# Feature sums and mean subtraction of the last layer norm, moved to TensorE for one column range

## The chip, the cores and the metric

The kernel runs on one core of a Trainium2 chip. The metric is the device time of one execution in microseconds (us). A NeuronCore has a matrix engine (TensorE, PE in the profile, with its weight loads listed as PEld), three engines for elementwise work (VectorE or DVE, ScalarE or ACT, GpSimd or POOL), and queues that issue transfers (SP is the main one here). Each engine runs its own list of instructions in order; semaphores make one wait for another.

## What is computed

One transformer-like layer (three parallel mixing heads, an output projection, layer norm, a SwiGLU feed-forward block, layer norm), for 1024 prompt tokens and 32 sample tokens with 1024 features. The change touches only the very last step, the second layer norm:

```python
def _layer_norm(x, g, b):
    xf = x.astype(jnp.float32)
    mu = xf.mean(-1, keepdims=True)
    var = jnp.square(xf - mu).mean(-1, keepdims=True)
    return ((xf - mu) * lax.rsqrt(var + LN_EPS) * g + b).astype(x.dtype)
...
    y = (jax.nn.silu(h @ w_gate) * (h @ w_up)) @ w_down
    x = _layer_norm(ALPHA * x + (1 + g2) * y, ln2_g, ln2_b)
```

The sums run over the 1024 features of each token.

## The kernel before, in words

Activations lie transposed: features on the 128 partitions, tokens along the free dimension. The 1024 features are eight feature tiles, called m or k below, from 0 to 7. The 1056 tokens are two groups: group 0 has tokens 0 to 511, group 1 has the other 544. Group 1 is worked in two column ranges of 272 tokens, (0, 272) and (272, 544). The array `z` holds the residual sum of a group, eight tiles of 272 columns for each range.

The matrix products use a two-part split of each operand (high and low part), so that each product of 128x128 weights with 272 columns is three matmuls (lines 117 to 119, `gemm`). These operands have the type fp32r. A matmul on plain fp32 operands, as the norm uses, shows in the profile as two matmul records.

The tail of the program is the loop at lines 1453 to 1469. It goes through the two column ranges in the order (272, 544), then (0, 272). For each it makes the last part of the up projection (`up`, line 1016), the last part of the down projection (`down`, line 1162) and the norm (`ln2`, line 1177).

`down` goes through the eight feature tiles in the order 4, 5, 6, 7, 0, 1, 2, 3. For each it issues twelve matmuls into a PSUM bank (tags "g" and "gu" in turn, three banks each) and then calls `sublayer_end` (line 951). There VectorE adds the gated product to `z` (line 960), and `ln_sum` (line 849) collects the sums of the norm:

- ScalarE squares the tile (line 853 for the first, line 856 for the others);
- GpSimd adds the tile to `zs`, the sum of the features (line 860);
- VectorE adds the square to `qs`, the sum of squares (line 862).

In the second range, (0, 272), the last two tiles of the order, 2 and 3, are "late": they are not added on GpSimd and VectorE but kept in a list (line 858) for TensorE.

`ln_means` (line 864) then sums over the partitions. TensorE multiplies `onesm`, a 128x128 matrix with 1/1024 in each place, with `zs` and with the kept tiles for the mean, and with `qs` and the kept squares for the mean square (line 872): six fp32 matmuls in the second range, two in the first. The results are `pm` and `pq`, in two PSUM banks of the tag "t".

`ln2` forms the variance on VectorE (line 1187) from `pq` and the square of `pm` (ScalarE, line 1185), copies `pm` to SBUF as `mean` (ScalarE, line 1186), and gets `r`, one over the deviation, from `ln_rstd` (lines 879 to 883: a logarithm and an exponential on ScalarE, then three VectorE steps). VectorE takes the mean off tile after tile (`less`, line 1189) and multiplies by `r` (`scaled`, line 1205). The first three `less` steps are placed right behind the variance; each later one is placed behind the `scaled` step of the tile before. Last comes the affine step with gain and offset, on ScalarE (line 1207), or for tile 7 of the last range on VectorE (line 1209). Tiles are stored (line 1212) in pairs 0-1, 2-3 and 4-5 and then singly, from SP's queue, except tile 6 of the last range, which goes from ScalarE's queue.

While `down` works on the second range, `weave` and the argument `turns` let the norm of the first range run tile by tile between its steps. The order of instructions on an engine is made ahead of the run by a planner that takes the program's order as priority and moves up a later instruction where an earlier one isn't ready by its own estimate. `issue_after` holds an instruction behind a named one of the same engine.

Of the kernel before, what the change touches and what calls it, by code (L numbers as in the profile page):

```python
# [7 lines left out]
F32 = mybir.dt.float32  # L8
F32R = mybir.dt.float32r
AF = mybir.ActivationFunctionType  # L10
ALU = mybir.AluOpType
# [4 lines left out]
P = 128  # L16
D = 1024
KT = 8
# [38 lines left out]
def weave(*parts):  # L57

    parts = list(parts)
    while parts:  # L60
        for p in list(parts):
            if next(p, parts) is parts:
                parts.remove(p)
# [6 lines left out]
class Kernel:  # L70
# [10 lines left out]
    def t(self, pool, shape, dt=F32, tag=None, bufs=None):  # L81
        self.n += 1
        kw = {} if bufs is None else {"bufs": bufs}
        return pool.tile(shape, dt, tag=tag, name=f"{self.phase}_{tag}_{self.n}", **kw)
# [751 lines left out]
    def ln_begin(self, eng, pivot=True, sum=True):  # L836
        t = lambda tag: self.t(self.pn, [P, 544], F32, tag, 2)
        return {"zs": t("zs"), "qs": t("qs"), "pv": t("pv"), "eng": eng, "pivot": pivot, "sum": sum,
                "order": range(KT), "late": (), "rest": []}

    def ln_pivot(self, st, z, sl):
        nc = self.nc
# [6 lines left out]
    def ln_sum(self, st, z, m, sl):  # L849
        nc = self.nc  # L850
        o = st["order"]
        if m == o[0]:
            nc.scalar.activation(st["qs"][:, sl], z[:, m, sl], AF.Square)
            return
        sq = self.t(self.p2, [P, 272], F32, "tmp", 4)[:, :sl.stop - sl.start]
        nc.scalar.activation(sq, z[:, m, sl], AF.Square)
        if m in st["late"]:
            st["rest"].append((z[:, m, sl], sq))
            return
        st["eng"].tensor_tensor(st["zs"][:, sl], z[:, o[0], sl] if m == o[1] else st["zs"][:, sl],  # L860
                              z[:, m, sl], ALU.add)
        nc.vector.tensor_tensor(st["qs"][:, sl], st["qs"][:, sl], sq, ALU.add)

    def ln_means(self, st, sl):


        out = []
        for i, x in enumerate(("zs", "qs")):
            p = self.t(self.pt, [P, 512], F32, "t")[:, :sl.stop - sl.start]
            parts = [st[x][:, sl]] + [y[i] for y in st["rest"]]  # L870
            for n, y in enumerate(parts):
                self.nc.tensor.matmul(p, self.onesm, y, start=n == 0, stop=n == len(parts) - 1)
            out.append(p)
        st["rest"] = []
        return out
# [301 lines left out]
    def ln2(self, c, st, a, b, aff, late=False):  # L1177

        self.phase = f"lnb{c}"
        nc, z, sl = self.nc, self.z[c], slice(a, b)  # L1180
        eng = {"p": nc.gpsimd, "v": nc.vector}
        pm, pq = self.ln_means(st, sl)
        mean = st["zs"][:, sl]
        v = self.t(self.p2, [P, 272], F32, "tmp", 4)[:, :b - a]
        nc.scalar.activation(v, pm, AF.Square)
        nc.scalar.copy(mean, pm)
        first = nc.vector.scalar_tensor_tensor(v, pq, self.epsa, v, ALU.add, ALU.subtract)
        r = st["pv"][:, sl]
        less = lambda k: nc.vector.tensor_tensor(z[:, k, sl], z[:, k, sl], mean, ALU.subtract)
        scale = self.ln_rstd(r, v)  # L1190
        if late:
            with self.tc.issue_after(first.ins):
                for k in range(3):
                    less(k)
        yield
        for k in range(KT):
            self.phase = f"lnb{c}"
            zk = z[:, k, sl]
            g, o = self.colp[:, 64 + k:65 + k], self.colp[:, 72 + k:73 + k]
            if not late:  # L1200
                less(k)
            elif k >= 3:
                with self.tc.issue_after(scaled.ins):
                    less(k)
            scaled = nc.vector.tensor_tensor(zk, zk, r, ALU.mult)
            if aff[k] == "a":
                nc.scalar.activation(zk, zk, AF.Identity, bias=o, scale=g)
            else:
                eng[aff[k]].tensor_scalar(zk, zk, g, o, ALU.mult, ALU.add)
            k0 = k if k >= 6 and c else k - k % 2  # L1210
            if k % 2 or k0 == k and k >= 6 and c:
                (nc.scalar if k in self.scq else nc.sync).dma_start(
                    self.d["o_yT"][k0:k + 1, :, GO[c] + a:GO[c] + b].rearrange("k p n -> p k n"), z[:, k0:k + 1, sl])
            yield
# [15 lines left out]
    def run(self):  # L1230
        nc, tc, d = self.nc, self.tc, self.d
        dr = self.pool("dr", space=DRAM)
        t = lambda shape, tag: self.t(dr, shape, F32, tag)
# [49 lines left out]
        sl = ExitStack()  # L1283
        self.pl = self.pada = self.pool("pl", ctx=sl)
        w1 = d["w_in_v"]
        rest = list(range(16, 20)) + list(range(8, 16))
# [71 lines left out]
        st = self.ln_begin(nc.gpsimd)  # L1358
# [18 lines left out]
        for g, (j0, nj) in enumerate(GROUPS):  # L1377
# [30 lines left out]
            if g == WOB - 1:  # L1408
                st = self.ln_begin(nc.gpsimd, sum=False)
# [20 lines left out]
        for g, (j0, nj) in enumerate(GROUPS):  # L1430
# [13 lines left out]
            if g < last:  # L1444
                st = self.ln_begin(nc.gpsimd, sum=False) if g == last - 1 else None
# [3 lines left out]
        n = nj * 256  # L1449
        t = self.t(self.pz, [P, 4, n], F32R, "z0", 1)  # L1450
        w = self.last_weights(((t[:, 0], t[:, 1]), (t[:, 2], t[:, 3])), (2, 3))
        act2 = dict(act)
        for half, (a, b) in enumerate(LN[1][::-1]):
            if half == 0:
                wt = {j: self.up_weights(j) for j in range(FF - TS, FF)}
            for j in range(FF - TS, FF):
                weave(self.up(1, j, (act, act2)[half], pa, ((a, b),), wt[j]))
            if half:
                st["late"] = st["order"][6:]
            else:  # L1460
                h, l = (self.t(pb, [P, KT * 272], F32R, f"{x}{a}", 1) for x in ("ah", "al"))
                w.update(self.last_weights(((h[:, :n], l[:, :n]), (h[:, n:2 * n], l[:, n:2 * n])), (0, 1)))
            self.down(1, last, (act, act2)[half], ((a, b),), st, w, end if half else iter(()))
            self.scq = (6,) if half else ()
            end = self.ln2(1, st, a, b, TAFF[half], True)
            if half:
                weave(end)
            else:
                next(end)
# [103 lines left out]
```

## Time and profile before

| quantity | value |
| --- | --- |
| time, median of 3 runs | 1392.73 us (1391.56 to 1393.49) |
| the profiled execution: time | 1390.37 us |
| the profiled execution: span, first to last instruction | 1388.5 us |
| mean granted TensorE clock | 0.993 of full speed |
| TensorE matmul busy | 1345.2 us, 97% |
| VectorE busy | 1034.2 us, 74% |
| ScalarE busy | 641.3 us, 46% |
| GpSimd busy | 259.1 us, 19% |

In the views quoted below a row of the timeline gives the start in us from the start of the span, the duration in us, the engine, the line, the operation, the tile written, the tiles read, the shapes and a count; a bracket names the idle time before it and what ended it. Rows with a count above one are merged: the duration then reaches from the first start to the last end. Starts of rows in line can lie closer than a duration, since an engine begins one instruction while the last drains; the distance from start to start is called the pitch below. Prefixes of tile names (`wo_z`, `sup_zs`, `lnb_t`) name the stage in which a buffer was made: `wo_z` is `z` of group 1, `sup_zs` and `sup_qs` are `zs` and `qs`, `sup_pv` is `r`, `lnb_t` is `pm` or `pq`, `dn_tmp` is a square.

### The profile page before, as it was taken

What the parts mean: (1) busy time and instruction counts of PE and PEld (TensorE: products, weight loads), DVE (VectorE), ACT (ScalarE), POOL (GpSimd) and SP (SyncE); (2) the same over time, 40 slices, a digit from 0 to 9 for tenths busy, and PEclk for the clock granted to TensorE, in tenths of its full rate; (3) what the DMA queues carried; (4) which work ended last, traced back from release to release, by engine and by line L of the source; (5) the groups of instructions that cost most, each with busy time, mean ns of one, the idle gap of its engine ahead of it and who ended that gap; (6) DMA issues with size and microseconds to landing.
All of it is one profiled execution on the core that took longest, in us unless ns stands there. A gap on an engine that the chain in (4) does not pass through costs nothing.

```text
span 1388.5 us, 25995 instructions
## 1 busy us (share of the span) xinstructions
PE 1345.2 (97%) x9683; PEld 1236.4 (89%) x9683; DVE 1034.2 (74%) x2214; ACT 641.3 (46%) x1261; POOL 259.1 (19%) x292
## 2 busy tenths in 40 slices
PE   7999999999999799999999999999999999999996
PEld 4899988899899778888887889899999999999996
DVE  5548656678689657777776766677898988888777
ACT  3323234444455444545544445335574544545355
POOL 0103200052157500000000000264610000000341
PEclk9999999999999899999999999999999999999998
DMA  9754577575665665444443442664497767453321
GB/s 362 266 211 134 176 242 212 187 237 149 212 205 160 180 184 182 125 131 137 133 135 86 108 127 81 195 169 134 157 229 195 216 163 214 136 175 115 101 90 65
DMA packets 136373, 233.09 MB, mean 168 GB/s; under 512 B 22564, under 2 KB 79532, under 8 KB 136248
## 3 DMA queue, kind: packets, MB, share of 16 engines
q1 hardware_dynamic: 130936, 221.34, 50.7%
q0 software_dynamic: 5168, 9.96, 4.7%
q8 instruction: 76, 1.25, 0.4%
q14 instruction: 49, 0.40, 0.1%
q10 hardware_dynamic: 144, 0.14, 0.0%
HBM read 197.50 MB, written 53.81 MB: 181 GB/s over the span
## 4 chain that ended last, share of the span: by engine, by line
PE 67%; DVE 5%; DMA 3%; ACT 1%; issue 1%; SPq 0%; POOL 0%; DVEq 0%; ACTq 0%
PE up_g L117 5%; PE up_g L118 5%; PE up_g L119 5%; PE dn_g L119 4%; PE dn_g L117 4%; PE dn_g L118 4%; PE sup_u L119 3%; PE sup_u L117 3%; PE sup_u L118 3%; PE wo_g L119 2%; PE wo_g L117 2%; PE wo_g L118 2%; PE sup_g L118 2%; PE sup_g L119 2%; PE sup_g L117 2%; PE fox_t L738 2%
## 5 line engine op out<-in xcount | busy, mean ns | idle before, releaser
L117 PE MATMUL up_g<-mlstm_ah,up_whi 128*128 128x512 f32 (+1 forms) x384 | 141.7, 369 | 4.4 <-ACT lna_tmp L981 3.3
L118 PE MATMUL up_g<-mlstm_al,up_whi 128*128 128x512 f32 (+1 forms) x384 | 142.1, 370 | 0.4 <-DVE mlstm_al L986 0.4
L119 PE MATMUL up_g<-mlstm_ah,up_wlo 128*128 128x512 f32 (+1 forms) x384 | 141.1, 368 | 0.0
L282 PE MATMUL tm_g<-tm_whi,start_h1h 128*128 128x256 f32 (+1 forms) x384 | 109.7, 287 | 1.5 <-ACT tm_mixs L633 1.5
L284 PE MATMUL tm_g<-tm_whi,start_h1l 128*128 128x256 f32 (+1 forms) x384 | 109.6, 287 | 0.0
L283 PE MATMUL tm_g<-tm_wlo,start_h1h 128*128 128x256 f32 (+1 forms) x384 | 109.5, 286 | 0.0
L117 PE MATMUL fm_g<-start_h1h,fm_whi 128*128 128x256 f32 (+2 forms) x344 | 101.7, 301 | 6.1 <-DVE fm_qkl L367 2.6
L118 PE MATMUL fm_g<-start_h1l,fm_whi 128*128 128x256 f32 (+2 forms) x344 | 100.8, 293 | 0.0
L119 PE MATMUL fm_g<-start_h1h,fm_wlo 128*128 128x256 f32 (+2 forms) x344 | 100.0, 292 | 0.0
L1105 ACT CAST sup_whi<-sup_raw 128x1024 fp32r<-128x1024 f32 x54 | 56.0, 1048 | 91.5 <-PE dn_u L118 47.9
L117 PEld LDWEIGHTS up_g<-mlstm_ah,up_whi 128*128 128x128 f32 x384 | 73.5, 192 | 16.7 <-ACT mlstm_ah L985 3.5
L118 PEld LDWEIGHTS up_g<-mlstm_al,up_whi 128*128 128x128 f32 x384 | 73.7, 192 | 12.3 <-DVE mlstm_al L986 1.5
L119 PEld LDWEIGHTS up_g<-mlstm_ah,up_wlo 128*128 128x128 f32 x384 | 73.8, 192 | 10.6
L105 ACT CAST up_whi<-up_raw 128x1024 fp32r<-128x1024 f32 x50 | 52.4, 1048 | 63.9 <-PE dn_g L118 25.1
L711 ACT ACTIVATE fox_p<-fox_s,fox_fmx 128x384 f32<-128x384 f32 (+2 forms) x96 | 55.0, 578 | 57.1 <-DVE fox_fmx L709 44.0
L282 PEld LDWEIGHTS tm_g<-tm_whi,start_h1h 128*128 128x128 f32 x384 | 72.2, 189 | 4.4 <-ACT tm_mixs L633 2.1
L117 PEld LDWEIGHTS fm_g<-start_h1h,fm_whi 128*128 128x128 f32 x344 | 64.7, 190 | 12.5 <-DVE fm_qkl L367 3.5
L1106 DVE TENSOR_TENSOR sup_wlo<-sup_raw,sup_whi 128x1024 fp32r<-128x1024 f32 x54 | 67.8, 1259 | 10.5 <-ACT sup_whi L1105 10.5
L106 DVE TENSOR_TENSOR up_wlo<-up_raw,up_whi 128x1024 fp32r<-128x1024 f32 x50 | 66.8, 1336 | 10.4 <-ACT up_whi L105 9.6
L284 PEld LDWEIGHTS tm_g<-tm_whi,start_h1l 128*128 128x128 f32 x384 | 72.2, 188 | 1.5 <-issue 1.2
L117 PE MATMUL dn_g<-up_acth,dn_whi 128*128 128x512 f32 (+2 forms) x200 | 73.5, 368 | 0.0
L118 PE MATMUL dn_g<-up_actl,dn_whi 128*128 128x512 f32 (+2 forms) x200 | 73.3, 368 | 0.0
(591 smaller groups left out, 4594.5 us busy)
## 6 DMA issues: line engine op xcount, KB each, us to landing
up_raw<-w_gu SPq DMA_DIRECT2D x50, 512.0 KB
dn_raw<-w_dn SPq DMA_DIRECT2D x28, 512.0 KB
ada_late<-w_ada SPq DMA_DIRECT2D x24, 512.0 KB
wo_raw<-w_o SPq DMA_DIRECT2D x24, 512.0 KB
sup_raw<-w_gu SPq DMA_DIRECT2D x20, 512.0 KB
start_dp<-w_gu SPq DMA_DIRECT2D x19, 512.0 KB
start_dp<-w_gu POOLq DMA_DIRECT2D x19, 512.0 KB, 7.8
sup_raw<-start_dp SPq DMA_DIRECT2D x18, 512.0 KB
```

Of the source, the lines that this page charges most:

```text
L105: nc.scalar.copy(hi[:, :w], raw[:, :w])
L106: (eng or nc.vector).tensor_tensor(lo[:, :w], raw[:, :w], f(hi[:, :w]), ALU.subtract)
L117: nc.tensor.matmul(ps, hi, xh(k), start=start and k == 0, stop=False)
L118: nc.tensor.matmul(ps, hi, xl(k), start=False, stop=False)
L119: nc.tensor.matmul(ps, lo, xh(k), start=False, stop=stop and k == n - 1)
L282: nc.tensor.matmul(ps[:, :ncol], xh, hi, start=k == 0, stop=False)
L283: nc.tensor.matmul(ps[:, :ncol], xh, lo, start=False, stop=False)
L284: nc.tensor.matmul(ps[:, :ncol], xl, hi, start=False, stop=k == 7)
L711: nc.scalar.activation(pr[:, lo:hi], banks[x][:, :hi - lo], AF.Exp, bias=mxs[:, 0:1], accum_out=sums[:, x:x + 1])
L738: nc.tensor.transpose(ps[:, c:c + P], probs[y][:, b * P:(b + 1) * P], self.ident)
L1105: nc.scalar.copy(h, x)
L1106: tt(l, x, f(h), ALU.subtract)
```

## The change

A flag `onpe` is set for the second range, (0, 272), alone. With it

- `ln_sum` no longer adds tiles on GpSimd. TensorE multiplies each tile with `onesm` and accumulates in one PSUM bank, `pm`, which is held from the first tile on. The matmul for a tile is issued after the product of the next tile.
- `ln_means` issues only the matmul of the last tile for the mean, and those of the mean square as before.
- `ln2` writes the mean with its sign turned. The first three tiles get the negative mean added on VectorE, as before with a subtraction. For tiles 3 to 7 TensorE forms the centred tile in a PSUM bank with two fp32 matmuls by the identity, one of the tile and one of the negative mean. VectorE's multiplication by `r` then reads that bank.
- For every range the copy of the mean is now an activation of the kind Copy with a scale of 1 or -1.

```diff
@@ ln_sum
         o = st["order"]
+        if st["onpe"]:
+            if m == o[0]:
+                st["pm"] = self.t(self.pt, [P, 512], F32, "t")[:, :sl.stop - sl.start]
+            for x in st["wait"]:
+                nc.tensor.matmul(st["pm"], self.onesm, x, start=x is st["first"], stop=False)
+            st["wait"] = [z[:, m, sl]]
+            if m == o[0]:
+                st["first"] = st["wait"][0]
...
-        st["eng"].tensor_tensor(st["zs"][:, sl], z[:, o[0], sl] if m == o[1] else st["zs"][:, sl],
-                              z[:, m, sl], ALU.add)
+        if not st["onpe"]:
+            st["eng"].tensor_tensor(st["zs"][:, sl], z[:, o[0], sl] if m == o[1] else st["zs"][:, sl],
+                                  z[:, m, sl], ALU.add)
         nc.vector.tensor_tensor(st["qs"][:, sl], st["qs"][:, sl], sq, ALU.add)
@@ ln_means
-        for i, x in enumerate(("zs", "qs")):
+        if st["onpe"]:
+            for n, x in enumerate(st["wait"]):
+                self.nc.tensor.matmul(st["pm"], self.onesm, x, start=False, stop=n == len(st["wait"]) - 1)
+            out.append(st["pm"])
+        for i, x in list(enumerate(("zs", "qs")))[len(out):]:
@@ ln2
-        nc.scalar.copy(mean, pm)
+        onpe = st["onpe"]
+        nc.scalar.activation(mean, pm, AF.Copy, scale=-1.0 if onpe else 1.0)
...
+        centred = {}
+        if onpe:
+            for k in range(3, KT):
+                p = centred[k] = self.t((self.pg, self.pu)[k % 2], [P, 512], F32, self.utag[k % 2])[:, :b - a]
+                nc.tensor.matmul(p, self.ident, z[:, k, sl], start=True, stop=False)
+                nc.tensor.matmul(p, self.ident, mean, start=False, stop=True)
...
-            elif k >= 3:
+            elif k >= 3 and not onpe:
                 with self.tc.issue_after(scaled.ins):
                     less(k)
-            scaled = nc.vector.tensor_tensor(zk, zk, r, ALU.mult)
+            scaled = nc.vector.tensor_tensor(zk, centred.get(k, zk), r, ALU.mult)
@@ run
             if half:
                 st["late"] = st["order"][6:]
+                st["onpe"] = True
```

More of the change, by code (lines that the diff above doesn't have):

```diff
@@ L838, in ln_begin @@
         return {"zs": t("zs"), "qs": t("qs"), "pv": t("pv"), "eng": eng, "pivot": pivot, "sum": sum,
-                "order": range(KT), "late": (), "rest": []}
+                "order": range(KT), "late": (), "rest": [], "onpe": False, "wait": [], "first": None}
     def ln_pivot(self, st, z, sl):
@@ L1185, in ln2 @@
         nc.scalar.activation(v, pm, AF.Square)
-        nc.scalar.copy(mean, pm)
+        onpe = st["onpe"]
+        nc.scalar.activation(mean, pm, AF.Copy, scale=-1.0 if onpe else 1.0)
         first = nc.vector.scalar_tensor_tensor(v, pq, self.epsa, v, ALU.add, ALU.subtract)
         r = st["pv"][:, sl]
-        less = lambda k: nc.vector.tensor_tensor(z[:, k, sl], z[:, k, sl], mean, ALU.subtract)
+        less = lambda k: nc.vector.tensor_tensor(z[:, k, sl], z[:, k, sl], mean, ALU.add if onpe else ALU.subtract)
         scale = self.ln_rstd(r, v)
```

## The prediction

> **What bounds the kernel now.** First the page's head, then a table of stretches of the last 35 us (each engine's busy us and count, the granted clock, DMA share, GB/s).
>
> ```profile
> span 1388.5 us, 25995 instructions
> PE 1345.2 (97%) x9683; PEld 1236.4 (89%) x9683; DVE 1034.2 (74%) x2214; ACT 641.3 (46%) x1261; POOL 259.1 (19%) x292
> ...
> 1354.00:1366.00 12.00, 12.00 (x95) 11.84 (x94) 9.26 (x24) 6.59 (x15) 1.69 (x3) 1.00 0.07 25
> 1366.00:1373.00 7.00, 7.00 (x57) 6.89 (x55) 7.00 (x14) 4.07 (x10) 3.97 (x5) 1.00 0.28 100
> 1373.00:1377.06 4.06, 3.65 (x13) 2.03 (x12) 2.10 (x5) 1.57 (x5) 0.19 (x1) 1.00 0.10 34
> 1377.06:1385.70 8.64, 0.00 (x0) 0.00 (x0) 8.32 (x21) 5.04 (x10) 0.00 (x0) 0.71 0.25 85
> ```
>
> TensorE is busy for 97% of the span, and through all 19 us of the last products; only then does it thin out and stop. So the stretch has three parts: products, on TensorE; sums, to 1377.06; normalising, on VectorE (8.32 of 8.64 us), and a last store. What TensorE is given before 1373 lengthens the program; what VectorE is relieved of after 1377 can shorten it. TensorE's timeline shows the hinge and the price of an fp32 matmul.
>
> ```profile
> 1358.05 0.62 PE L872 MATMUL lnb_t<-sup_zs,start_onesm 128*128 128x272 f32 x2
> 1358.50 0.62 PE L872 MATMUL lnb_t<-sup_qs,start_onesm 128*128 128x272 f32 x2
> ...
> 1372.82 0.28 PE L119 MATMUL dn_u<-up_acth,up_al 128*128 128x272 f32 x1
> 1373.24 0.73 PE L872 MATMUL lnb_t<-sup_zs,start_onesm 128*128 128x272 f32 x2
> 1374.85 0.72 PE L872 MATMUL lnb_t<-sup_qs,start_onesm 128*128 128x272 f32 x2 [0.17 <-DVE sup_qs L862]
> 1375.41 0.62 PE L872 MATMUL lnb_t<-dn_tmp,start_onesm 128*128 128x272 f32 x2
> 1375.87 0.62 PE L872 MATMUL lnb_t<-wo_z,start_onesm 128*128 128x272 f32 x2
> 1376.33 0.62 PE L872 MATMUL lnb_t<-dn_tmp,start_onesm 128*128 128x272 f32 x2
> ```
>
> The products' last matmul starts at 1372.82, and with the usual pitch of 0.13 the next could start at 1372.95. Each L872 row is one fp32 matmul (two records) of 272 columns; in line they stand 0.45 to 0.46 apart (1358.05 to 1358.50, 1375.41 to 1375.87 to 1376.33). That is the price I use: 0.46. TensorE waits here: six times 0.46 is 2.76, but from 1372.95 to the end of the sixth, 1376.33 + 0.46, pass 3.84. The waits are for VectorE, which is late:
>
> ```profile
> 1365.82 0.50 DVE L960 SCALAR_TENSOR_TENSOR wo_z<-dn_g,start_mod,wo_z 128x272 f32<-128x272 f32 x1
> 1366.23 0.50 DVE L960 SCALAR_TENSOR_TENSOR wo_z<-dn_u,start_mod,wo_z 128x272 f32<-128x272 f32 x1
> 1367.05 0.84 DVE L1205 TENSOR_TENSOR wo_z<-wo_z,sup_pv 128x272 f32<-128x272 f32 x1
> 1367.81 1.01 DVE L1189 TENSOR_TENSOR wo_z<-wo_z,sup_zs 128x272 f32<-128x272 f32 x1
> 1370.44 1.00 DVE L1189 TENSOR_TENSOR wo_z<-wo_z,sup_zs 128x272 f32<-128x272 f32 x1
> 1372.48 1.01 DVE L862 TENSOR_TENSOR sup_qs<-sup_qs,dn_tmp 128x272 f32<-128x272 f32 x1
> 1374.71 0.49 DVE L960 SCALAR_TENSOR_TENSOR wo_z<-dn_u,start_mod,wo_z 128x272 f32<-128x272 f32 x1
> ```
>
> ```profile
> 1367.67 0.86 POOL L860 TENSOR_TENSOR sup_zs<-sup_zs,wo_z 128x272 f32<-128x272 f32 x1
> 1369.38 1.76 POOL L860 TENSOR_TENSOR sup_zs<-sup_zs,wo_z 128x272 f32<-128x272 f32 x2 [0.85 <-DVE wo_z L960]
> 1372.35 0.84 POOL L860 TENSOR_TENSOR sup_zs<-sup_zs,wo_z 128x272 f32<-128x272 f32 x1 [1.21 <-DVE wo_z L960]
> ```
>
> The last tile reaches `z` at 1374.71, 1.76 after the products ended. VectorE steps that lie under a GpSimd sum take 0.84 to 1.01 us; the same steps alone take 0.43 (the L1189 row at 1381.02, next).
>
> ```profile
> 1377.06 0.50 DVE L1187 SCALAR_TENSOR_TENSOR lnb_tmp<-lnb_t,start_epsa,lnb_tmp 128x272 f32<-128x272 f32 x1 [1.85 <-ACT lnb_tmp L1185]
> 1379.95 1.15 DVE L1205 TENSOR_TENSOR wo_z<-wo_z,sup_pv 128x272 f32<-128x272 f32 x3
> 1381.02 0.43 DVE L1189 TENSOR_TENSOR wo_z<-wo_z,sup_zs 128x272 f32<-128x272 f32 x1
> 1381.48 0.44 DVE L1205 TENSOR_TENSOR wo_z<-wo_z,sup_pv 128x272 f32<-128x272 f32 x1
> 1384.80 0.44 DVE L1205 TENSOR_TENSOR wo_z<-wo_z,sup_pv 128x272 f32<-128x272 f32 x1
> 1385.27 0.42 DVE L1209 TENSOR_SCALAR wo_z<-wo_z,start_colp 128x272 f32<-128x272 f32 x1
> ```
>
> ```profile
> 1375.30 0.43 ACT L856 ACTIVATE dn_tmp<-wo_z 128x272 f32<-128x272 f32 x1 [0.88 <-DVE wo_z L960]
> 1380.43 2.14 ACT L1207 ACTIVATE wo_z<-wo_z,start_colp 128x272 f32<-128x272 f32 x4 [1.94 <-DVE wo_z L1205]
> 1384.44 0.61 ACT L1207 ACTIVATE wo_z<-wo_z,start_colp 128x272 f32<-128x272 f32 x1 [0.22 <-DVE wo_z L1205]
> 1385.09 0.38 ACTq L1212 DMA_DIRECT2D o_yT<-wo_z  x1
> ```
>
> From 1381.02 on VectorE alternates: mean off, times `r`, 0.83 us a tile ((1384.80 - 1381.48) / 4), and ScalarE waits 0.22 for it before each tile. Tile 7 ends at 1385.69, and its store goes out:
>
> ```profile
> 1384.25 0.37 SPq L1212 DMA_DIRECT2D o_yT<-wo_z  x1
> 1385.72 0.34 SPq L1212 DMA_DIRECT2D o_yT<-wo_z  x1
> ...
> GB/s 322 339 270 35 0 0 0 0 0 226 331 348 331 322 348 331 296 287 305 209 87 331 383 279 44 0 0 0 0 0 0 0 0 0 0 0 0 0 0 0
> ```
>
> The last line is the stretch 1384 to 1389 in 40 slices of 0.125 us. Data of the pair issued at 1384.25 move from slice 9 (1385.13), 0.88 later. All three last stores, four tiles of 128 x 272 x 4 bytes, 557 thousand bytes, are through by 1387.1, with a dip at 1386.4 to 1386.6 before tile 7's bytes. Full slices show about 330 GB/s. The span ends 1.4 later, 2.78 after the last issue.
>
> **The change part by part.**
>
> *Feature sums on TensorE.* Five GpSimd additions go. Eight fp32 matmuls for the mean replace three (`zs` and two late tiles). By the order of issue six of the eight (tiles 4, 5, 6, 7, 0, 1) stand in front of the end of the last product; each finds its tile in `z` by then, since a tile has a whole product (twelve times 0.125, 1.5 us) and more to get there. TensorE has no hole to hide them in: 12.00 of 12.00 and 7.00 of 7.00 busy. So the products end at 1372.95 + 6 x 0.46 = 1375.71. Behind them stand tile 2, tile 3, and the three sums of squares. Tile 3 gets into `z` about 0.2 + 0.49 later, its square 0.45 after that, so at 1376.4 and 1376.9; `qs` has long been ready, as VectorE, with 0.4 to 0.6 us back on each of the four slow steps above, is no longer late. Tile 2, `qs` and the first square fill the time. The fifth matmul starts at 1375.71 + 4 x 0.46 = 1377.55, against 1376.33: **+1.22 us**. The variance step follows as before, 0.73 behind that start (1376.33 to 1377.06), at 1378.28. Bounds: with tile 3 ahead of the squares TensorE waits 0.3 more, +1.5; nothing less than +1.2 is left unless TensorE has room that the table of stretches denies (a rival). VectorE's gain from GpSimd's silence, 0.41 + 0.58 + 0.57 + 0.58 = 2.1 us, buys nothing where TensorE comes last.
>
> *Mean with its sign turned.* One ScalarE step for one, of the length of the ScalarE steps on 272 columns above (0.43 to 0.61) or less. The mean's sum now ends two matmuls ahead of the squares' sum, so the copy lies under those: nothing. In the first range and group 0 only the kind of the copy changes: nothing, at most some 0.05 each, under products.
>
> *Centring by the identity.* Ten fp32 matmuls, 4.6 us, on a TensorE that is idle in the row of 1377.06 to 1385.70. In order behind the sums they run from 1378.01; pair n is done 0.92n later, plus about 0.2 to drain: tile 3 at 1379.1, tile 7 at 1382.8. VectorE, three `scaled` steps after its first at 1379.95 + 1.22 = 1381.17, asks for tile 3 at 1382.25 and for tile 7 some 1.64 later. Cover enough, 1.1 us at the least; if it went, each missing microsecond would be paid in full. PSUM banks: three of "gu" and two of "g", each type has three, and the products are done with them.
>
> *VectorE without five subtractions.* A step that reads PSUM:
>
> ```profile
> L1036 DVE TENSOR_TENSOR up_sil<-up_g,up_sil x35: 410/442/692, 472.5 to 1358.6; 128x512 f32<-128x512 f32 x17, 128x256 f32<-128x256 f32 x10, 128x272 f32<-128x272 f32 x8
> ```
>
> 0.44 at the median, against 0.43 from SBUF; back to back PSUM steps have a pitch of 0.41 (1365.82 to 1366.23). So a tile costs 0.41 instead of 0.83, five tiles save 2.1 on VectorE. Next is ScalarE: four affine steps in 2.14 with the last 0.61 long, a pitch of 0.51. From 1380.43 + 1.22 = 1381.65 its seven tiles end at 1381.65 + 6 x 0.51 + 0.61 = 1385.32; VectorE's tile 7 ends earlier, at 1384.77. Pair 4-5 is ready at 1384.81 and goes out at 1384.83, 0.58 later than before; then tile 7 at 1385.2 and tile 6 at 1385.34, close together. So the transfers bind: 0.88 to the first byte, 557 thousand bytes at 331 GB/s is 1.68, and 1.4 to the end of the span: 1388.8. Taken by the last issue alone, 1385.34 + 2.78, it would be 1388.1.
>
> *Sum.* Sums +1.22; normalising and stores -0.92 (the end, 1388.8, stands 3.97 behind the issue at 1384.83, where it stood 4.25 behind 1384.25; that is 0.28 back from the store, and 0.64 from ScalarE's pair 4-5). Together **+0.3 us**: the profiled execution would be 1390.7. It lay 2.4 under the median of the runs, so the median goes from 1392.7 to 1393.0. About 0.2%, 2.8 us, is what a measurement of this kernel can tell from no change.
>
> **The rivals.**
>
> *B, VectorE decides the sums: faster.* If TensorE could take in the six matmuls without ending later, VectorE's lateness would be what goes: the variance would come at the earliest 1372.95 + 0.22 + 0.49 + 0.45 + 0.73 = 1374.84, 2.2 earlier, and with 0.92 from the tail the time is 3.1 less, 1389.6. Against it: the products have a pitch of 0.125 without a gap. The Trainium skill (SBUF — State Buffer, the section on two separate sides) says that GpSimd and a VectorE step with two SBUF inputs lock each other out for a whole instruction; the slow VectorE rows agree, and by that rule alone the change would look like this gain.
>
> *C, the planner moves identity matmuls ahead of the sums: slower.* They need only finished tiles, and the planner does reorder: the sum of tile 3 (1375.87) stands behind two sums of squares, though the code has it in front of them. Each one moved up costs 0.46 before the variance and saves nothing later. All five of the tiles: +2.3, in all +2.6, 1395.3. It decides from the point where the planner sees TensorE wait before the last two sums; five sums in line leave little wait. One or two moved up is as likely as five.
>
> *D, TensorE's clock halves before the centring: slower.* The row
>
> ```profile
> 1381.00:1382.00 1.00, 0.00 (x0) 0.00 (x0) 0.96 (x4) 1.00 (x4) 0.00 (x0) 0.50 0.00 0
> ```
>
> has a clock of 0.50, four us after the last matmul. At half speed the ten matmuls take 9.2 instead of 4.6, tile 7 comes at 1387.2, and the end at about 1391.0: +2.5, 1395.2. It needs several idle microseconds first, and I see 0.3. The Trainium skill (TensorE: Matmul & The Clock Gate, Part 1) puts the halving after about 3.4 us of idleness; the trace agrees (1.00 in 1373.00:1377.06, 0.50 from 1381).
>
> *E, another plan from the changed copy on.* TensorE's whole idle time is 43 us (1388.5 - 1345.2), so a new order can hardly win; it can lose or win one to three us.
>
> **How the numbers follow.** The forecast, +0.3 with its own range from -0.7 (the last issue alone) to +1.2 (waits, one matmul moved up), has 0.66; C 0.16; D 0.02; B 0.06; E 0.10, evenly spread. Over 2.8 us slower: the dearer half of C with waits on top, half of D and 0.03 of E: 0.11. Over 2.8 faster: B and 0.02 of E less what falls short: 0.06. Within: 0.83. The range takes in C but not all of D, and half of the way to B: 1391.5 to 1395.3.
>
> **What would show it.** Seven `onesm` matmuls among or right behind the products, the last product near 1375.7; no GpSimd sums after 1366 and VectorE steps back at 0.43; five `scaled` steps 0.41 apart; ScalarE's affine steps without waits; variance 1.2 later; last issues bunched within 0.6 us. I am wrong if the products end where they did, if identity matmuls stand ahead of the last sum, or if `scaled` waits for TensorE.

## The result

With the change the median of 15 runs is 1397.97 us; the kernel before has 1394.37 over 15 runs made beside them. The ratio is 1.0027, with a 95% interval from 1.0017 to 1.0037: the change makes the kernel slower, by 2.4 to 5.2 us. The prediction said 1393.0, within 0.2% of before, and had 1395.3 as its upper end. (The kernel before itself came out at 1392.73 in the three runs that the prediction had, at 1394.4 to 1396.5 in the later ones.)

The page's head of the changed kernel, and its table of three stretches (columns as before):

```profile
span 1399.1 us, 26046 instructions
PE 1354.6 (97%) x9713; PEld 1244.7 (89%) x9713; DVE 1032.3 (74%) x2209; ACT 641.6 (46%) x1261; POOL 253.0 (18%) x287
...
1374.00:1384.00 10.00, 10.00 (x71) 9.48 (x70) 6.77 (x18) 4.74 (x11) 0.00 (x0) 1.00 0.24 85
1384.00:1388.58 4.58, 4.58 (x22) 3.80 (x21) 0.43 (x1) 1.11 (x3) 0.00 (x0) 1.00 0.00 0
1388.58:1395.62 7.04, 2.19 (x10) 1.48 (x8) 6.10 (x16) 4.50 (x9) 0.00 (x0) 1.00 0.20 67
```

GpSimd does nothing in the last 21 us, as intended. But TensorE is now busy for the whole 4.58 us from 1384 to the variance step at 1388.58; from the products' end to the variance the forecast had 2.6 in all (1375.71 to 1378.28).

Two profiles differ by 10.6 us in span, and most of that isn't the change. Up to the first sum matmul of the range (272, 544) both traces list the same instructions in the same order on every engine, but for two copies of the mean for group 0, which ScalarE now makes as activations. Yet the first sums of the first layer norm start 8.4 us later in one profile than in the other:

```profile
L872 PE MATMUL lna_t<-wo_zs,start_onesm x8: 377/384/392, 433.6 to 974.7; 128*128 128x256 f32 x4, 128*128 128x272 f32 x4
```

```profile
L886 PE MATMUL lna_t<-wo_zs,start_onesm x8: 377/384/392, 442.0 to 983.0; 128*128 128x256 f32 x4, 128*128 128x272 f32 x4
```

(Minimum, median and maximum duration in ns, then first and last start.) So I measure from a fixed instruction, that first sum matmul, and call it the anchor: at 1358.05 before, and in the profile after (the view is cut behind the first of its two records)

```profile
1366.11 0.39 PE L886 MATMUL lnb_t<-sup_zs,start_onesm 128*128 128x272 f32 x1
```

The *tail*, from the anchor to the end of the span, is 30.45 us before (1388.5 - 1358.05) and 32.99 with the change: **2.54 us longer**. But for the two copies that is all that the change touches, and it lies in the interval of the runs, near its lower end. Over the profiles in the table below the anchor stands anywhere between 1358.05 and 1369.36, with the same instructions ahead of it.

Where the 2.54 us come from, in TensorE's timeline of the changed kernel from the products' last matmul on:

```profile
1383.60 0.29 PE L119 MATMUL dn_u<-up_acth,up_al 128*128 128x272 f32 x1
1383.73 0.62 PE L886 MATMUL lnb_t<-sup_qs,start_onesm 128*128 128x272 f32 x2
1384.19 1.08 PE L1215 MATMUL lnb_g<-wo_z,start_ident 128*128 128x272 f32 x4
1385.10 0.62 PE L857 MATMUL dn_t<-wo_z,start_onesm 128*128 128x272 f32 x2
1385.56 0.62 PE L886 MATMUL lnb_t<-dn_tmp,start_onesm 128*128 128x272 f32 x2
1386.02 0.62 PE L880 MATMUL dn_t<-wo_z,start_onesm 128*128 128x272 f32 x2
1386.48 1.54 PE L1215 MATMUL lnb_u<-wo_z,start_ident 128*128 128x272 f32 x6
1387.85 0.62 PE L886 MATMUL lnb_t<-dn_tmp,start_onesm 128*128 128x272 f32 x2
1388.31 0.62 PE L1216 MATMUL lnb_u<-sup_zs,start_ident 128*128 128x272 f32 x2
```

L857, L880 and L886 are sums over features; L1215 is the identity matmul of a tile, L1216 that of the mean. Two tiles (x4 records) go through the identity right behind the sum of `qs`, at 1384.19, and three more (x6) at 1386.48, ahead of the last sum, which the variance waits for. Five times 0.46 us stand between the products and the variance that the variance doesn't need. VectorE in the same stretch:

```profile
1375.47 0.43 DVE L1204 TENSOR_TENSOR wo_z<-wo_z,sup_zs 128x272 f32<-128x272 f32 x1
1381.97 0.50 DVE L974 SCALAR_TENSOR_TENSOR wo_z<-dn_g,start_mod,wo_z 128x272 f32<-128x272 f32 x1 [0.93 <-PE dn_g L119]
1383.93 0.50 DVE L974 SCALAR_TENSOR_TENSOR wo_z<-dn_u,start_mod,wo_z 128x272 f32<-128x272 f32 x1 [1.46 <-PE dn_u L119]
1388.58 0.50 DVE L1202 SCALAR_TENSOR_TENSOR lnb_tmp<-lnb_t,start_epsa,lnb_tmp 128x272 f32<-128x272 f32 x1 [4.15 <-PE lnb_t L886]
1391.47 1.15 DVE L1226 TENSOR_TENSOR wo_z<-wo_z,sup_pv 128x272 f32<-128x272 f32 x3
1392.54 0.43 DVE L1226 TENSOR_TENSOR wo_z<-lnb_u,sup_pv 128x272 f32<-128x272 f32 x1
1393.93 0.43 DVE L1226 TENSOR_TENSOR wo_z<-lnb_u,sup_pv 128x272 f32<-128x272 f32 x1
1394.40 0.42 DVE L1230 TENSOR_SCALAR wo_z<-wo_z,start_colp 128x272 f32<-128x272 f32 x1
```

VectorE is no longer slow (0.43 at 1375.47, where the same step took 1.01 before) nor late: the last two tiles, 2 and 3, enter `z` at 1381.97 and 1383.93, the latter 0.2 after the products' end. Then it waits 4.15 us. Behind the variance the centred tiles come at a pitch of 0.35. ScalarE and the last stores:

```profile
1391.95 3.64 ACT L1228 ACTIVATE wo_z<-wo_z,start_colp 128x272 f32<-128x272 f32 x7 [1.94 <-DVE wo_z L1226]
1395.62 0.37 ACTq L1233 DMA_DIRECT2D o_yT<-wo_z  x1
```

Seven affine steps in one row without a wait. From variance to end of span the profile after has 10.5 us (1399.1 - 1388.58), before 11.4 (1388.5 - 1377.06): the second half of the change gained 0.9 us, as computed.

### The profile page after: what moved, and what is told of

Same layout as the page of the kernel before. It is cut to its first block, busy times and chain, and to the rows that moved or that the text cites. A ratio compares the mean times of both kernels' runs of the same rounds, so it can differ in the third digit from the quotient of the medians.

```text
span 1399.1 us, 26046 instructions
## 1 busy us (share of the span) xinstructions
PE 1354.6 (97%) x9713; PEld 1244.7 (89%) x9713; DVE 1032.3 (74%) x2209; ACT 641.6 (46%) x1261; POOL 253.0 (18%) x287
## 4 chain that ended last, share of the span: by engine, by line
PE 79%; DMA 9%; DVE 6%; ACT 3%; issue 2%; SPq 1%; POOL 0%; DVEq 0%; ACTq 0%
PE up_g L117 5%; PE up_g L118 5%; PE up_g L119 5%; PE dn_g L119 4%; PE dn_g L117 4%; PE dn_g L118 4%; PE sup_u L119 3%; PE sup_u L117 3%; PE sup_u L118 3%; PE tm_g L282 2%; PE tm_g L284 2%; PE tm_g L283 2%; PE wo_g L118 2%; PE wo_g L117 2%; PE wo_g L119 2%; PE sup_g L118 2%
## 5 line engine op out<-in xcount | busy, mean ns | idle before, releaser
L119 PEld LDWEIGHTS up_g<-mlstm_ah,up_wlo 128*128 128x128 f32 x384 | 73.4, 191 | 10.6
L1120 DVE TENSOR_TENSOR sup_wlo<-sup_raw,sup_whi 128x1024 fp32r<-128x1024 f32 x54 | 67.9, 1260 | 10.5 <-ACT sup_whi L1119 10.5
L283 PEld LDWEIGHTS tm_g<-tm_wlo,start_h1h 128*128 128x128 f32 x384 | 72.8, 190 | 0.6 <-issue 0.4
```

The costliest lines, as they stand in the source:

```text
L119: nc.tensor.matmul(ps, lo, xh(k), start=False, stop=stop and k == n - 1)
L283: nc.tensor.matmul(ps[:, :ncol], xh, lo, start=False, stop=False)
L1120: tt(l, x, f(h), ALU.subtract)
```

## The experiments

All are measured by the tail, since the instructions ahead of the anchor are the same, as above. Spans are printed to 0.1 us, so a tail is good to 0.05. e5 and e6 were run once, for the profile, and have no ratio against before. The table gives the anchor and the span of each profile; then, counted from the anchor, the start of the last sum of squares of the second range and of the variance step; and the tail, span less anchor. The first row of the timelines quoted for e1 to e5 and for e9 is the anchor.

| kernel | anchor | span | last sum | variance | tail, us | against before |
| --- | --- | --- | --- | --- | --- | --- |
| before | 1358.05 | 1388.5 | 18.28 | 19.01 | 30.45 | |
| the change | 1366.11 | 1399.1 | 21.74 | 22.47 | 32.99 | +2.54 |
| e1: change, identity matmuls held | 1361.12 | 1391.8 | 19.45 | 20.18 | 30.68 | +0.23 |
| e2: feature sums only | 1369.04 | 1400.7 | 19.45 | 20.18 | 31.66 | +1.21 |
| e3: centring only, not held | 1367.64 | 1398.5 | 19.67 | 20.40 | 30.86 | +0.41 |
| e4: centring only, held | 1365.33 | 1394.8 | 18.28 | 19.01 | 29.47 | -0.98 |
| e5: change, two of five free | 1366.74 | 1398.4 | 20.36 | 21.10 | 31.66 | +1.21 |
| e6: as e4, four GpSimd sums left out | 1365.27 | 1393.7 | 17.19 | 17.92 | 28.43 | -2.02 |
| e7: as e4, sums on VectorE | 1369.36 | 1399.3 | 18.74 | 19.48 | 29.94 | -0.51 |
| e8: as e7, tiles stored singly | 1364.17 | 1394.2 | 18.74 | 19.48 | 30.03 | -0.42 |
| e9: as e7, tile 1 summed on TensorE | 1363.61 | 1392.7 | 17.85 | 18.58 | 29.09 | -1.36 |
| e10: as e4, tiles 0 and 1 summed on TensorE | 1365.85 | 1395.2 | 18.11 | 18.83 | 29.35 | -1.10 |

### e1: the whole change, the identity matmuls held behind the last sum

```diff
-                self.nc.tensor.matmul(p, self.onesm, y, start=n == 0, stop=n == len(parts) - 1)
+                self.lastsum = self.nc.tensor.matmul(p, self.onesm, y, start=n == 0, stop=n == len(parts) - 1)
...
-                nc.tensor.matmul(p, self.ident, z[:, k, sl], start=True, stop=False)
-                nc.tensor.matmul(p, self.ident, mean, start=False, stop=True)
+                with self.tc.issue_after(self.lastsum.ins):
+                    nc.tensor.matmul(p, self.ident, z[:, k, sl], start=True, stop=False)
+                    nc.tensor.matmul(p, self.ident, mean, start=False, stop=True)
```

> The whole change, with the identity matmuls held behind the last sum over features; nothing else differs. The measure is the tail, from the first sum matmul of the range (272, 544) to the end of the span: 30.5 us before (1358.05 to 1388.5), 33.0 with the change (1366.11 to 1399.1); all instructions ahead of it are the same. Theory M (identity matmuls moved ahead of the last sum delay the variance, five times 0.46): the tail becomes 30.5 + 1.2 - 0.9 = 30.8, 2.2 shorter than with the change, and the time is that of before within 0.1%. Rival S (the feature sums among the products are the whole cost): the tail stays at 32.5 or more and the time 0.2% over before.

```profile
1361.12 0.39 PE L886 MATMUL lnb_t<-sup_zs,start_onesm 128*128 128x272 f32 x1
1378.73 0.62 PE L886 MATMUL lnb_t<-sup_qs,start_onesm 128*128 128x272 f32 x2
1380.57 0.62 PE L886 MATMUL lnb_t<-dn_tmp,start_onesm 128*128 128x272 f32 x2
1381.03 0.62 PE L1216 MATMUL lnb_u<-wo_z,start_ident 128*128 128x272 f32 x2
```

TensorE's timeline: five sums in line from 1378.73 to 1380.57, and the first identity matmul only behind them. The tail is 30.68, 2.31 shorter than with the change: five times 0.46. The time against before has a ratio of 0.9998 (0.9984 to 1.0011). The order of the identity matmuls is the cause of nearly all of the loss.

### e2 to e4: the two halves, each alone

In e2 the feature sums stay on TensorE and VectorE takes the mean off; in e3 and e4 it is the other way round, with the identity matmuls free (e3) or held as in e1 (e4).

```diff
 e2:
-        onpe = st["onpe"]
+        onpe = False
 e3, e4:
-                st["onpe"] = True
+                st["cent"] = True
...
-        onpe = st["onpe"]
+        onpe = st.get("cent", False)
```

> The feature sums on TensorE alone; the mean is taken off by VectorE as before. Theory M: the sums cost 1.2 us and nothing gives it back: the tail is 31.7, half-way between before (30.5) and the change (33.0). Rival S: 33.0 or more, since the centring would have saved something in the change. Rival G (VectorE without GpSimd beside it decides): 29.5 or less.

> The centring on TensorE alone, the feature sums on GpSimd as before; the identity matmuls stand where the planner puts them: two right behind the products, three ahead of the last sum of squares. Theory M: the first two lie in TensorE's waits (1.1 us of them before), the three put the variance back by 1.3, the tail's end gives 0.9: 30.8. If their place doesn't matter (rival S): 29.5.

> The centring alone with the identity matmuls held behind the last sum. Theory M: variance as before, 0.9 gained behind it: the tail is 29.5 and the time 0.07% under before. If reading the centred tiles from PSUM or the bunched stores eat the gain: 30.3 to 30.5.

TensorE's timeline of e2 and of e4, anchor and last sum, and in e4 the identity matmul behind it:

```profile
1369.04 0.39 PE L886 MATMUL lnb_t<-sup_zs,start_onesm 128*128 128x272 f32 x1
1388.49 0.62 PE L886 MATMUL lnb_t<-dn_tmp,start_onesm 128*128 128x272 f32 x2
```

```profile
1365.33 0.39 PE L886 MATMUL lnb_t<-sup_zs,start_onesm 128*128 128x272 f32 x1
1383.61 0.62 PE L886 MATMUL lnb_t<-dn_tmp,start_onesm 128*128 128x272 f32 x2
1384.07 0.62 PE L1216 MATMUL lnb_u<-wo_z,start_ident 128*128 128x272 f32 x2
```

The sums alone cost 1.21 us, the held centring alone gains 0.98; the two add up to the +0.23 of e1. The ratios of the runs are 1.0012 (0.9996 to 1.0028) and 0.9991 (0.9979 to 1.0004): of the right sign, but not clear of 1. In e3 the five identity matmuls are moved as well:

```profile
1367.64 0.39 PE L886 MATMUL lnb_t<-sup_zs,start_onesm 128*128 128x272 f32 x1
1384.46 0.73 PE L886 MATMUL lnb_t<-sup_qs,start_onesm 128*128 128x272 f32 x2
1385.94 1.54 PE L1215 MATMUL lnb_u<-wo_z,start_ident 128*128 128x272 f32 x6
1387.31 0.62 PE L886 MATMUL lnb_t<-dn_tmp,start_onesm 128*128 128x272 f32 x2
```

Three stand ahead of the last sum (1385.94) and put the variance back by 1.39; the two that stand right behind the products fill a time in which TensorE waited anyway, and cost nothing. The tail is 30.86, the ratio 1.0009 (0.999 to 1.0028). So a moved identity matmul costs its 0.46 only where TensorE has other work; with the feature sums in its line, all five find it.

### e5: two of the five left free

```diff
+                with ExitStack() as held:
+                    if k not in (4, 6):
+                        held.enter_context(self.tc.issue_after(self.lastsum.ins))
```

> The whole change, but only the identity matmuls of tiles 4 and 6 are left free to move; those of tiles 3, 5 and 7 are held behind the last sum. Theory M (each moved one costs its 0.46): the tail is that of all held, 30.68, plus 0.92, 31.6; with five moved it was 32.99. If only the last three, which stand right ahead of the last sum, did harm: 30.7.

TensorE's timeline:

```profile
1366.74 0.39 PE L886 MATMUL lnb_t<-sup_zs,start_onesm 128*128 128x272 f32 x1
1384.81 1.08 PE L1218 MATMUL lnb_g<-wo_z,start_ident 128*128 128x272 f32 x4
1387.10 0.62 PE L886 MATMUL lnb_t<-dn_tmp,start_onesm 128*128 128x272 f32 x2
```

The two go through the identity at 1384.81 (x4 records), in the place that they have in the change. Tail 31.66: 0.98 over e1 with two moved, 2.31 with five. The price goes with the number.

### e6 to e10: what GpSimd's sums cost

e6 leaves out four of the five GpSimd additions of the second range, so its mean lacks four tiles; the rest is e4.

```diff
-        if not st["onpe"]:
+        if not st.get("cent") or m == o[1]:
             st["eng"].tensor_tensor(st["zs"][:, sl], ...
```

> As the centring held (tail 29.47), but four of the five GpSimd additions of the second range are left out, so that the mean lacks four tiles. What it asks: how much GpSimd's sums cost VectorE and the variance. If VectorE's lateness is the limit of the sums and TensorE the next: no VectorE step over 0.5 us in the stretch, the six sums in line behind the products, variance 1.3 earlier, tail 28.2. If VectorE's slow steps hide elsewhere: 29.4.

TensorE's timeline, from the products' last matmul on:

```profile
1380.05 0.28 PE L119 MATMUL dn_u<-up_acth,up_al 128*128 128x272 f32 x1
1380.17 0.62 PE L886 MATMUL lnb_t<-sup_zs,start_onesm 128*128 128x272 f32 x2
1382.46 0.62 PE L886 MATMUL lnb_t<-dn_tmp,start_onesm 128*128 128x272 f32 x2
```

With four of GpSimd's five additions gone the six sums stand in line, from 1380.17 to 1382.46, right behind the products. The variance comes 1.09 earlier than in e4, where 1.3 was expected; the tail is 28.43. So VectorE's lateness under GpSimd's sums cost 1.1 us before the change. Of VectorE's steps on two SBUF tiles in the second range one is still slow, 0.84 us at 1374.28, and it lies under the one addition that is left (1374.03, 0.79 us); the others that stand singly in the timeline take 0.43. This agrees with what the Trainium skill (SBUF — State Buffer, the section on two separate sides) says of the two engines, that GpSimd and a VectorE step with two SBUF inputs lock each other out for a whole instruction. How much of it lies on the path is 1.1 us and not the 2.1 of the slow steps. e7 gives the five additions to VectorE, and e8 stores each tile alone as well:

```diff
 e7:
+                st["eng"] = nc.vector
 e8:
-            k0 = k if k >= 6 and c else k - k % 2
-            if k % 2 or k0 == k and k >= 6 and c:
+            one = 0 if onpe else 6
+            k0 = k if k >= one and c else k - k % 2
+            if k % 2 or k0 == k and k >= one and c:
```

> As the centring held (29.47), with the five feature sums of the second range made by VectorE instead of GpSimd: five steps of 0.36 more for VectorE, 2.1 less of slow steps. Theory M with VectorE late in the sums: the variance comes 0.4 to 0.7 earlier, tail 28.8 to 29.1, the time 0.1% under before. If the steps cost VectorE as much as GpSimd's presence did: 29.4 to 29.6.

> As the one with VectorE's sums, and each tile of the second range stored by itself instead of in pairs. If the transfers of the last stores are in line (the tiles' bytes at 330 GB/s, one queue behind another), an earlier start shortens the end by 0.4 to 0.6: tail 28.3 to 28.6. If the last issue alone counts: no change against pairs.

VectorE's timeline of e7 at the end of the products, and TensorE's:

```profile
1384.45 0.50 DVE L974 SCALAR_TENSOR_TENSOR wo_z<-dn_u,start_mod,wo_z 128x272 f32<-128x272 f32 x1 [0.15 <-PE dn_u L119]
1385.22 0.43 DVE L870 TENSOR_TENSOR sup_zs<-sup_zs,wo_z 128x272 f32<-128x272 f32 x1
```

```profile
1385.71 0.73 PE L886 MATMUL lnb_t<-sup_zs,start_onesm 128*128 128x272 f32 x2 [1.29 <-DVE sup_zs L870]
```

Both missed. VectorE makes the last addition behind the last tile's step, and TensorE waits 1.29 for `zs`: the variance is 0.47 later, not earlier. Their ratios are 1.0006 (0.9993 to 1.0019) and 0.9995 (0.998 to 1.0009). Single stores gave nothing (30.03 against 29.94), although they moved the data earlier: counted from the variance step, the first bytes move at 4.8 us in e8 and 5.4 in e7, and the last are through at 8.8 and 9.1. The span ends 10.5 behind the variance in both. So the last byte alone doesn't set the end; what fills the 1.7 us behind it in e8, against 1.4 in e7, isn't settled. e9 takes that last addition off VectorE: TensorE sums tile 1 along with tiles 2 and 3, behind the products. e10 leaves the first three additions on GpSimd and gives tiles 0 and 1 to TensorE.

```diff
 e9:
+                st.update(eng=nc.vector, latez=st["order"][5:6], restz=[])
 e10:
+                st.update(latez=st["order"][4:6], restz=[])
 both:
-        if not st["onpe"]:
+        if m in st.get("latez", ()):
+            st["restz"].append(z[:, m, sl])
+        else:
             st["eng"].tensor_tensor(...)
...
-            parts = [st[x][:, sl]] + [y[i] for y in st["rest"]]
+            parts = [st[x][:, sl]] + (st.get("restz", []) if i == 0 else []) + [y[i] for y in st["rest"]]
```

> The centring held; VectorE makes the feature sums of tiles 4, 5, 6, 7 and 0, and tile 1 goes to TensorE with tiles 2 and 3. With all five additions on VectorE the last one came behind the last tile and TensorE waited 1.3 us for it; here it stands ahead of the last tile. If that wait was the loss: seven sums nearly in line, variance 0.3 to 0.6 earlier than with GpSimd's sums (19.01 behind the anchor), tail 28.9 to 29.2 against 29.47. If VectorE's additions cost what GpSimd's presence did: 29.4 or more.

> The centring held; GpSimd makes the feature sums of tiles 4 to 7 only, and tiles 0 and 1 go to TensorE with 2 and 3, behind the products. Eight sums in line, 2.0 us freed of GpSimd's late additions: variance 0.15 earlier than with five additions on GpSimd, tail 29.3. If GpSimd's early additions slow VectorE as much as the late ones: 29.9.

TensorE's timeline of e9:

```profile
1363.61 0.39 PE L888 MATMUL lnb_t<-sup_zs,start_onesm 128*128 128x272 f32 x1
1378.61 0.73 PE L888 MATMUL lnb_t<-sup_zs,start_onesm 128*128 128x272 f32 x2
1379.17 1.54 PE L888 MATMUL lnb_t<-wo_z,start_onesm 128*128 128x272 f32 x6
1381.01 1.08 PE L888 MATMUL lnb_t<-dn_tmp,start_onesm 128*128 128x272 f32 x4
```

Seven sums nearly in line from 1378.61. The tail of e9 is 29.09, 1.36 shorter than before and 3.9 shorter than with the change; that of e10 is 29.35. Both came out as written. e9 has the shortest tail of the kernels that do the whole work, but a gain of 0.1% doesn't show in the runs: its ratio against before is 0.9996 (0.998 to 1.0012), that of e10 1.0 (0.9984 to 1.0015).

## Why the prediction was wrong

The step that failed is the order behind the products: "Tile 2, `qs` and the first square fill the time. The fifth matmul starts at 1375.71 + 4 x 0.46 = 1377.55". In that place stand ten matmuls, not five: in the frame of before, the last sum starts at 1379.8 (21.74 behind the anchor, 1358.05 + 21.74). This is rival C, five identity matmuls moved ahead for +2.3 and in all +2.6; measured were +2.31 (the change against e1) and +2.54. The prediction named this mechanism and its price and gave it a chance of 0.16. The row that spoke for it was quoted (the planner had put the sum of tile 3 behind two sums of squares); against it stood only my own count that TensorE has work in that place, by the times of the trace. The planner orders by its own estimate, and that this agrees with the trace was assumed. Why it saw a wait there isn't settled: in the changed kernel the sum of tile 2 (1385.10) stands behind two identity matmuls although VectorE had ended tile 2 by 1382.5, 1.2 us before the products ended.

Of the 5.0 us between the forecast median of 1393.0 and the measured 1397.97 these five matmuls are 2.3. Another 1.6 are the kernel before, whose median was 1392.73 over the first three runs and 1394.37 over fifteen. The rest, about 1 us, is the difference between the 3.6 us of the two medians and the 2.54 of the tail, inside the interval of the runs.

The other terms:

- *Feature sums, products' end*: predicted +2.76 for six matmuls among the products. Their last matmul starts 17.49 behind the anchor (1383.60) instead of 14.77 (1372.82): +2.7. Right.
- *Feature sums, variance*: predicted +1.22; without the moved matmuls it is 20.18 - 19.01 = 1.17 (e1, e2). Right.
- *GpSimd's silence buys nothing where TensorE comes last*: right for the change. Rival B, by which VectorE's lateness would be what goes, put the whole of it at 2.2 us earlier; e6, which is that case without TensorE's additional sums, gave 1.09, since six sums in line then set the variance. B's 2.2 also left out its own price: five sums behind 1372.95 at 0.46 put the last at 1374.79 and the variance at 1375.52, 1.5 earlier.
- *Centring and stores*: predicted -0.92; e4 has -0.98. The size is right, in part by luck. PSUM steps came at a pitch of 0.35 and not 0.41, so tile 7 was ready early and its store went out first (1390.60 in e4), with pair 4-5 behind it (1391.04); the prediction had them the other way round, and began the last line of transfers with pair 4-5. The transfers do run in line at the end: in e4, over the 5 us from 1389.5 in slices of 0.125 us,

```profile
DMA  0079999991599999999999999999994000000000
GB/s 0 9 252 322 348 322 348 331 270 26 183 348 313 331 331 366 331 331 313 339 375 331 339 331 348 331 331 279 322 331 166 18 0 0 0 0 0 0 0 0
```

the engines are full from slice 11 (1390.88) to slice 29, at some 330 GB/s: the line is full before pair 4-5 is issued. The span ends 3.4 us behind the last issue, where it ended 2.8 behind it before, so the last issue alone doesn't set the end; by e8 an earlier line doesn't shorten it either, at least not one of single stores. What binds the end is not shown. The forecast's lower bound, -0.7 for "the last issue alone", was a slip: 1388.1 against 1388.5 is -0.4.

- *The sum*: +0.3 predicted, +0.23 in e1. The forecast was right for the kernel with the order that it assumed.
- *Rival D*: the clock stays at 1.00 through all identity matmuls, and those of the mean keep a pitch of 0.46. It didn't come up, since TensorE had no idle time ahead of them. The prediction's 3.4 us is no fixed delay here: behind the end of the last matmul the granted clock fell to 0.50 after 3.7 us before the change, and after 2.3 (e6) to 5.3 us (e1) in the other profiles.
- *Rival E*: up to the anchor nothing stands in another order.

How much a measurement tells depends on where it starts: the anchor moves by 11 us between profiles with the same instructions ahead of it, and the intervals of the runs are 2.8 to 5.3 us wide. The sum of +2.54 was visible in the runs; those of e1 to e4 only in the tail. Within the tail parts repeat to 0.01 us: the products' last matmul starts 14.78 us behind the anchor in before, e3, e4 and e6 to e10, where no feature sum stands among the products, and 17.49 in the change, e1, e2 and e5, where six do.

## What to carry to other kernels

Work that becomes ready early and is needed late needs a hold when it is given to the engine that sets the path: a planner that fills what it takes for a wait puts it ahead of the step that everything waits for, and each such instruction costs its full length there (0.46 us here, five of them), unless it fills a wait that is real (two of five in e3). Before an elementwise step is moved to TensorE, count the matmuls that stand between its last operand and the first result that others need, in the order that the planner makes. And where the runs scatter more than the effect, measure from an instruction in front of which nothing differs: a tail of 30 us resolved 0.1 us where the intervals of whole runs were 2.8 to 5.3 us wide.

## What the runs showed of the hardware

VectorE's product of a PSUM tile and an SBUF tile had a pitch of 0.35 us (1392.54 to 1393.93 for four), no longer than that of two SBUF tiles (0.36, from the three steps in 1.15 us at 1391.47); I had expected 0.41, from steps with a third operand. With GpSimd adding beside it VectorE's step of two SBUF tiles took up to 1.01 us, and 0.43 without; over the second range that lateness was worth 1.1 us of the time to the variance (e6). The first part of the program, the same instructions in all kernels but for the two copies, took between 1358 and 1369 us up to the anchor; between the two profiles compared above the whole difference was there by the first layer norm (433.6 and 442.0), and its cause wasn't looked for.
